# A hybrid diffusion step on one core: the split activations of the dense layers at other SBUF start addresses

## The chip, the cores and the metric

The kernel runs on one core of a Trainium2 chip. The metric is the device time of one execution in microseconds. The program has five instruction streams: PE (matmuls), its weight loads (PEld), DVE, ACT and POOL (elementwise work), and SP, which issues all DMAs. Of the kernel before there are three timed executions, and one more was taken with the hardware profiler.

## The reference

Two layers of a hybrid backbone over 384 tokens (128 of context and 256 latent ones), D_MODEL = 1024, all in float32. Per layer, cut to what matters here:

```
h   = rms_norm(x) * (1 + scale1) + shift1
u   = h @ w_in                          # 1024 -> 11328 columns
y0, y1, y2 = ssd(u), attention(u), mlstm(u)
out = sum_n(sigmoid(g_n) * (y_n @ w_branch[n])) @ w_out
x   = x + gate1 * out
h   = rms_norm(x) * (1 + scale2) + shift2
x   = x + gate2 * ((silu(a) * b) @ w_ffn_out)   # a, b = halves of h @ w_ffn_in
```

At the end there is one more rms_norm. The result must agree with a float32 computation, which decides how the matmuls are done.

## The kernel before, in words

**Dense products.** All activations lie transposed, [128 channels, 8 blocks of channels, 384 tokens]. A dense operand is held as two float32r tiles, an upper part (the value rounded by a copy to float32r) and a lower part (value minus upper part). Weights stream from HBM in pieces of 128x1024 (`raw`) and are split the same way by ACT (`wh`) and by DVE or POOL (`wl`), in `piece` (lines 700 to 729). A product is three matmuls: wh with the upper part, wh with the lower part, wl with the upper part. In the names of the trace the upper and lower parts are HH and HL (inputs of the mixers, of the second of the three branch projections and of the output projection), PH and PL (the first and the third branch projection), A and C (input of the FFN, 386 columns: two more carry the shift). They are all filled by `split_act`, `modulate` and `scaled`.

**Which operand moves.** In `dense_t` (line 736) the weights are stationary, 128 columns each, and the activations stream past, 384 or 386 columns; this is the form of nearly all work. In `dense_n` (line 774; queries, keys, values) the roles are changed: 128 tokens of HH or HL are stationary, and 512 columns of `wh` or `wl` stream. In the second FFN product (line 1553) the moving halves lie in D, E, F, B, HH and HL, by 4, 4, 4, 2, 4 and 4 blocks of the hidden dimension.

**The order.** All calls are recorded first; `Recorder.order` (line 409) then runs a small model of the engines (costs in line 367, priorities set by `urgency`) and writes every engine's instructions in the order that the model finds. Neither the model nor its table of buffers knows an address. `Engines`' instructions are all emitted in line 545, so every row of the trace has that line, and rows are told apart by tiles.

**Addresses.** Each buffer tag is one place in a pool, and pools lie one behind the other in SBUF, per partition in bytes: constants `cp`, pad p1, weights `wp` (raw, wh, wl), pad p2, `bp`, pad p3, `mp`, small buffers `sp`, rings `rp`. `PADS` sets the pads' sizes. `wp` begins at 21760, which is 85 x 256. All tags of `bp` and `mp` have sizes that are multiples of 256 bytes (12288, 6144, 12544, 14336 to 16384 and 15360), and a block of 384 columns is 1536 = 6 x 256 bytes, a row of A or C 448 x 4 = 7 x 256 bytes. So all blocks of one tag begin at one value modulo 256. Before, p2 = 64 puts A to F, PH and PL at 64; p3 = 192 puts HH and HL back to 0.

**Two places used below as measures.** The setup splits some of the first weight pieces not into `wp` but into A and E (`OPEN_HOMES`, line 584), which lie at 64 modulo 256: those matmuls have stationary weights at 64 and HH or HL at 0 as the moving part.

The functions touched and those that call them:

Of the kernel before, what the change touches and what calls it, by code (L numbers as in the profile page):

```python
# [17 lines left out]
D = 1024  # L18
# [47 lines left out]
def stream():  # L66

    s = [(("ada", 0, u), 4) for u in range(4)]
    for l in range(LAYERS):
        early = iter(gates())  # L70
        s += [(("gate", l) + next(early), 1) for _ in range(FIRST_GATES if l else 0)]
        s += [(("dtmg", l), 1)]
        base = [(("in", l, OFF[n] + j * P), 1) for n in ("sx", "sb", "sc") for j in range(2 if n != "sx" else 8)]
        base += [(("inn", l, OFF["aq"] + j * 512), 4) for j in range(3)]
        base += [(("in", l, OFF[n] + j * P), 1) for n in ("mq", "mk") for j in range(8)]
        base += [(("inn", l, OFF["mv"] + j * 512), 4) for j in range(2)]
        base += [(("in", l, OFF[n] + j * P), 1) for n in ("sz", "mo") for j in range(8)]
        main = []
        for i, it in enumerate(base):
            main += [(("gate", l) + next(early), 1) for at in EARLY_GATES[FIRST_GATES if l else 0:] if at == i]  # L80
            main += [it]
        main += [(("br", l, n, j), 1) for n, j in gates()]
        at = len(main) - ADA_OVER

        late = []
        for i in range(KT):
            late += [(("ada", 0, 1, i // 2), 4)] if i % 2 else []
            late += [(("adv", 0, SHIFT2, i), 1), (("adv", 0, GATE2, i), 1)]
        s += main if l else main[:at] + spread(main[at:], late)
        s += [(("out", l, j), 1) for j in range(8)]  # L90
        ff = [((n, l, j), 1) for j in range(FT) for n in ("fa", "fb")]
        fo = [(("fo", l, i), 1) for i in range(FT)]
        if l + 1 < LAYERS:
            blocks = [(("adv", l + 1, place, j), 1) for place in range(6) for j in range(8)]
            n = len(ff) - ADV_FROM
            at = len(blocks) * n // (n + len(fo))
            s += ff[:ADV_FROM] + spread(ff[ADV_FROM:], blocks[:at]) + spread(fo, blocks[at:])
        else:
            s += ff + fo
    return s  # L100
# [33 lines left out]
class Buf:  # L134


    def __init__(self, pool, shape, dtype, tag, bufs, name, ext=None):
        self.pool, self.shape, self.dtype, self.tag, self.bufs, self.name, self.ext = pool, shape, dtype, tag, bufs, name, ext
        self.real = ext
        self.psum = False  # L140
        self.writes, self.reads = [], []
        self.left, self.place, self.ends = 0, 0, {}
# [427 lines left out]
ND, NM, NL = 3, 4, 1  # L570


BIG = ("A", "B", "C", "D", "E", "F", "PH", "PL")
MOVED = ("HH", "HL")
PADS = dict(p1=96, p2=64, p3=192)

ROW = 448
NR = 4
# [17 lines left out]
class Net:  # L596
    def __init__(self, ctx, tc, I, O):
        self.tc = tc
        self.rec = Recorder()
        self.nc = Engines(self.rec)  # L600
        ext = lambda d: {k: View(Buf(None, tuple(v.shape), F32, None, None, k, ext=v)) for k, v in d.items()}
        self.I, self.O = ext(I), ext(O)
        e = ctx.enter_context
        PSUM, DRAM = bass.MemoryType.PSUM, bass.MemoryType.DRAM
        self.pools = {n: e(tc.tile_pool(name=n, bufs=1, **k)) for n, k in (
            ("cp", {}), ("p1", {}), ("wp", {}), ("p2", {}), ("bp", {}), ("p3", {}), ("mp", {}), ("sp", {}), ("rp", {}), ("pd", dict(space=PSUM)), ("pm", dict(space=PSUM)),
            ("pl", dict(space=PSUM)), ("dr", dict(space=DRAM)))}
        self.n = 0
        self.stream = stream()
        self.spos = 0  # L610
        self.ppos = 0
        self.turn = 0
# [7 lines left out]
        return self.buf("cp", name, shape, 1)  # L620

    def slot(self, tag, shape, dt=F32):
        return self.buf("bp" if tag in BIG else "mp" if tag in MOVED else "sp", tag, shape, 1, dt)

    def ring(self, tag, shape, bufs=2, dt=F32):
        return self.buf("rp", tag, shape, bufs, dt)
# [302 lines left out]
    def setup(self):  # L929
# [10 lines left out]
        for k in (0, KT // 2):  # L940
            self.dma(self.x[:, k:k + KT // 2], I["xT"][:, k:k + KT // 2])
        for n, size in PADS.items():
            if size:
# [835 lines left out]
```

## Time and profile before

| | us |
|---|---|
| median of 3 executions | 1867.72 |
| lowest, highest | 1866.60, 1870.51 |
| the profiled execution | 1869.78 |
| its span, first to last instruction | 1868.0 |
| PE busy in it | 1827.6 (98%) |
| weight loads busy | 1716.6 (92%) |
| DVE, ACT, POOL busy | 1411.8, 942.5, 380.6 |

A matmul's duration in the trace is longer than its share of the engine, because the next one starts while it drains. The time that a matmul costs in a run without a pause is the distance between starts: (start of the last minus start of the first) divided by the number of matmuls between. The granted clock was 1.00 in nearly the whole span, which is 2.4 GHz, so 384 columns alone are 160.0 ns.

### The profile page before, as it was taken

The numbers are of one execution on the slowest core, as the hardware profiler recorded it, in microseconds if no ns is written. First come the engines' busy times: TensorE is split into PE (matmuls) and PEld (weight loads), VectorE is DVE, ScalarE is ACT, GpSimd is POOL, SyncE is SP. The second block draws the span as 40 slices with busy tenths as digits, with TensorE's granted clock in tenths as the row PEclk, the third lists the DMA queues.
The fourth block names the chain that finished last, engine by engine and source line by source line (L and its number), as shares of the span: only waits on it lengthen the run. The fifth ranks groups of instructions, "written<-read, shape, count | busy, mean of one in ns | idle before, by whom it ended". The sixth has DMA issues, their size and how long they took to land. (4 is left out here: it accounts for less than half of the span.)

```text
span 1868.0 us, 30198 instructions
## 1 busy us (share of the span) xinstructions
PE 1827.6 (98%) x10888; PEld 1716.6 (92%) x10888; DVE 1411.8 (76%) x2988; ACT 942.5 (50%) x1905; POOL 380.6 (20%) x365
## 2 busy tenths in 40 slices
PE   6999999999999999999999999999999999999997
PEld 5998998788889999999999889977989999999996
DVE  5858866898879889999879788578987567666522
ACT  4555655666533444443356556556665334544431
POOL 0223311232012211214402233112310121000132
PEclk9999999999999999999999999999999999999998
DMA  9466444665398757676764764445644554444441
GB/s 338 143 177 181 134 133 140 149 175 158 123 349 291 238 166 218 219 230 202 232 201 138 177 170 126 139 129 150 190 122 150 172 157 156 129 128 126 124 125 57
DMA packets 118598, 320.42 MB, mean 172 GB/s; under 512 B 13872, under 2 KB 57264, under 8 KB 116528
## 3 DMA queue, kind: packets, MB, share of 16 engines
q1 hardware_dynamic: 118448, 318.49, 55.9%
q8 instruction: 86, 1.41, 0.3%
q14 instruction: 64, 0.52, 0.1%
HBM read 297.64 MB, written 19.75 MB: 170 GB/s over the span
## 5 line engine op out<-in xcount | busy, mean ns | idle before, releaser
L545 ACT ACTIVATE wh<-raw 128x1024 fp32r<-128x1024 f32 x372 | 393.8, 1059 | 524.8 <-PE d L545 454.5
L545 DVE TENSOR_TENSOR wl<-raw,wh 128x1024 fp32r<-128x1024 f32 x350 | 452.8, 1294 | 206.0 <-ACT wh L545 204.9
L545 PE MATMUL d<-HH,wh 128*128 128x384 f32 x1424 | 483.0, 346 | 0.0
L545 PE MATMUL d<-HL,wh 128*128 128x384 f32 x1424 | 466.4, 335 | 0.0
L545 PE MATMUL d<-HH,wl 128*128 128x384 f32 x1360 | 455.9, 335 | 0.0
L545 PEld LDWEIGHTS d<-HH,wh 128*128 128x128 f32 x1424 | 267.1, 188 | 13.8 <-issue 11.3
L545 PEld LDWEIGHTS d<-HL,wh 128*128 128x128 f32 x1424 | 267.0, 188 | 0.7
L545 PEld LDWEIGHTS d<-HH,wl 128*128 128x128 f32 x1360 | 255.3, 188 | 0.0
L545 PE MATMUL d<-A,wh 128*128 128x386 f32 x744 | 252.5, 339 | 0.4 <-DVE sc L545 0.4
L545 PE MATMUL d<-C,wh 128*128 128x386 f32 x744 | 251.2, 338 | 0.0
L545 PE MATMUL d<-A,wl 128*128 128x386 f32 x744 | 251.1, 338 | 0.0
L545 PEld LDWEIGHTS d<-A,wh 128*128 128x128 f32 x744 | 140.6, 189 | 1.1 <-issue 0.7
L545 PEld LDWEIGHTS d<-C,wh 128*128 128x128 f32 x744 | 140.7, 189 | 0.4
L545 PEld LDWEIGHTS d<-A,wl 128*128 128x128 f32 x744 | 140.6, 189 | 0.0
L545 POOL TENSOR_TENSOR sc<-sc,sc 128x126 f32<-128x126 f32 x112 | 61.8, 573 | 314.8 <-DVE sc L545 252.3
L545 POOL TENSOR_TENSOR wl<-raw,wh 128x1024 fp32r<-128x1024 f32 x22 | 55.9, 2543 | 269.5 <-ACT sh L545 190.2
L545 DVE SCALAR_TENSOR_TENSOR PH<-PL,n,cst 128x128 f32<-128x128 f32 x288 | 96.7, 370 | 10.8 <-DMA PL<-rowr 5.0
L545 PE MATMUL d<-wh,HH 128*128 128x512 f32 x240 | 97.8, 407 | 0.0
L545 PE MATMUL d<-wl,HH 128*128 128x512 f32 x240 | 93.9, 391 | 0.0
L545 PE MATMUL d<-wh,HL 128*128 128x512 f32 x240 | 93.7, 391 | 0.0
L545 PE MATMUL d<-PH,wh 128*128 128x384 f32 x256 | 86.7, 339 | 0.0
L545 PE MATMUL d<-PH,wl 128*128 128x384 f32 x256 | 86.2, 337 | 0.0
(283 smaller groups left out, 3200.9 us busy)
## 6 DMA issues: line engine op xcount, KB each, us to landing
raw<-in_ws SPq DMA_DIRECT2D x438, 512.0 KB, 3.8
PL<-rowr SPq DMA_DIRECT2D x48, 384.0 KB, 5.3
gd<-sc SPq DMA_DIRECT2D x48, 192.0 KB, 2.0
pb<-gd SPq DMA_DIRECT2D x48, 192.0 KB, 3.3
A<-in_ws SPq DMA_DIRECT2D x4, 1536.0 KB, 8.1
ex<-rowe SPq DMA_DIRECT2D x32, 128.0 KB, 3.9
ex<-rowe SPq DMA_DIRECT2D x16, 256.0 KB, 5.6
yad<-pb SPq DMA_DIRECT2D x16, 192.0 KB, 3.4
```

Source lines behind the costliest of these rows:

```text
L545: tc.keep_in_program_order(getattr(engines[op.eng], meth)(*[real(a) for a in args], **{k: real(v) for k, v in kw.items()}))
```

## The change

The tags of dense operands get a pool by a table, `HOME`. `bp` keeps B, D, E and F. The upper parts A, HH and PH go to a new pool `hp`, the lower parts C, HL and PL to `lp`. Four pads stand between the pools: p3 grows from 192 to 224 and p4 = 160 is new. By the sizes above, `wp` stays at 0 modulo 256 and `bp` at 64; `hp` begins at 64 + 224 = 288, which is 32 modulo 256, and `lp` at 32 + 160 = 192.

```
-BIG = ("A", "B", "C", "D", "E", "F", "PH", "PL")
-MOVED = ("HH", "HL")
-PADS = dict(p1=96, p2=64, p3=192)
+HOME = dict(B="bp", D="bp", E="bp", F="bp", A="hp", HH="hp", PH="hp", C="lp", HL="lp", PL="lp")
+PADS = dict(p1=96, p2=64, p3=224, p4=160)
...
-("cp", {}), ("p1", {}), ("wp", {}), ("p2", {}), ("bp", {}), ("p3", {}), ("mp", {}), ("sp", {}), ("rp", {}), ...
+("cp", {}), ("p1", {}), ("wp", {}), ("p2", {}), ("bp", {}), ("p3", {}), ("hp", {}), ("p4", {}), ("lp", {}), ("sp", {}), ("rp", {}), ...
...
-        return self.buf("bp" if tag in BIG else "mp" if tag in MOVED else "sp", tag, shape, 1, dt)
+        return self.buf(HOME.get(tag, "sp"), tag, shape, 1, dt)
```

The small buffers and the rings behind move up by 192 bytes in all. On PE, DVE, ACT and SP the two programs have the same instructions in the same order, with the same waits; only buffer numbers and addresses differ. POOL has one instruction more, at its start, where the pads are set to zero. Its list there before (p_6 to p_8 are the pads, `ones` and `silc` are constants):

```order
L545 MEMSET p_6_93 128x24
L545 MEMSET p_7_97 128x16
L545 MEMSET p_8_99 128x48
L545 MEMSET ones_101 128x128
L545 MEMSET silc_103 128x256
```

and with the change:

```order
L545 MEMSET p_6_99 128x24
L545 MEMSET p_7_103 128x16
L545 MEMSET p_8_105 128x56
L545 MEMSET p_9_107 128x40
L545 MEMSET ones_109 128x128
L545 MEMSET silc_113 128x256
```

One pad of 40 columns has come in ahead of `ones`, and the pad before it is 8 columns wider.

## Rows read from the trace of the kernel before

**Rows 1.** The page, part 1: engines' busy time, share of the span, instructions.
```profile
PE 1827.6 (98%) x10888; PEld 1716.6 (92%) x10888; DVE 1411.8 (76%) x2988; ACT 942.5 (50%) x1905; POOL 380.6 (20%) x365
```

**Rows 2.** Busy time by stretches: start:end, length, engines' busy time (instructions), granted clock, DMA.
```profile
540.00:860.00 320.00, 319.58 (x1846) 313.75 (x1846) 292.84 (x461) 136.29 (x249) 68.22 (x44) 1.00 0.72 235
1460.00:1780.00 320.00, 320.00 (x1838) 319.73 (x1837) 201.19 (x292) 141.68 (x252) 33.56 (x25) 1.00 0.46 140
```

**Rows 3.** The page, part 5: matmul groups, count | busy us, mean ns | idle before.
```profile
L545 PE MATMUL d<-HH,wh 128*128 128x384 f32 x1424 | 483.0, 346 | 0.0
L545 PE MATMUL d<-HL,wh 128*128 128x384 f32 x1424 | 466.4, 335 | 0.0
L545 PE MATMUL d<-HH,wl 128*128 128x384 f32 x1360 | 455.9, 335 | 0.0
L545 PE MATMUL d<-A,wh 128*128 128x386 f32 x744 | 252.5, 339 | 0.4 <-DVE sc L545 0.4
L545 PE MATMUL d<-C,wh 128*128 128x386 f32 x744 | 251.2, 338 | 0.0
L545 PE MATMUL d<-A,wl 128*128 128x386 f32 x744 | 251.1, 338 | 0.0
L545 PE MATMUL d<-wh,HH 128*128 128x512 f32 x240 | 97.8, 407 | 0.0
L545 PE MATMUL d<-PH,wh 128*128 128x384 f32 x256 | 86.7, 339 | 0.0
L545 PE MATMUL d<-PL,wh 128*128 128x384 f32 x256 | 86.2, 337 | 0.0
```

**Rows 4.** Timeline of PE, moving HH and HL at 0, weights at 0: start, us.
```profile
247.84 0.33 PE L545 MATMUL d<-HH,wh 128*128 128x384 f32 x1
...
250.96 0.81 PE L545 MATMUL m<-C,D 128*128 128x256 f32 x4
```

**Rows 5.** Timeline of PE, moving PH and PL at 64, weights at 0.
```profile
523.58 0.34 PE L545 MATMUL d<-PH,wh 128*128 128x384 f32 x1
...
525.66 0.34 PE L545 MATMUL d<-PH,wh 128*128 128x384 f32 x1
```

**Rows 6.** Timeline of PE, FFN: moving A and C at 64, 386 columns.
```profile
851.51 0.34 PE L545 MATMUL d<-A,wh 128*128 128x386 f32 x1
...
855.71 0.51 PE L545 MATMUL d<-D,wh 128*128 128x384 f32 x2
```

**Rows 7.** Timeline of PE, `dense_n`: stationary HH and HL at 0, 512 columns.
```profile
153.91 0.39 PE L545 MATMUL d<-wh,HH 128*128 128x512 f32 x1
...
157.31 0.39 PE L545 MATMUL d<-wh,HH 128*128 128x512 f32 x1
```

**Rows 8.** Timeline of PE, stationary weights in E at 64, moving HH, HL at 0.
```profile
48.26 0.34 PE L545 MATMUL m<-HH,E 128*128 128x384 f32 x1
...
52.50 0.33 PE L545 MATMUL d<-HH,wh 128*128 128x384 f32 x1
```

**Rows 9.** Timeline of PE, HH and HL resuming behind three transposes.
```profile
241.11 0.49 PE L545 MATMUL m<-cst,pb 128*128 128x128 f32 x3
241.35 0.42 PE L545 MATMUL d<-HH,wh 128*128 128x384 f32 x1
241.61 0.33 PE L545 MATMUL d<-HL,wh 128*128 128x384 f32 x1
...
242.50 0.33 PE L545 MATMUL d<-HH,wh 128*128 128x384 f32 x1
```

**Rows 10.** Timeline of PE, second FFN product: B (64), then HH (0), then HL (0).
```profile
872.89 0.51 PE L545 MATMUL d<-B,wh 128*128 128x384 f32 x2
...
873.93 0.51 PE L545 MATMUL d<-HH,wh 128*128 128x384 f32 x2
...
875.51 0.51 PE L545 MATMUL d<-HL,wh 128*128 128x384 f32 x2
```

**Rows 11.** Groups of ACT: two squares of one shape, written to `sc` (128) and `nacc` (96).
```profile
L545 ACT ACTIVATE sc<-PH 128x384 f32<-128x384 f32 x35 | 17.6, 516 | 22.0 <-DVE PH L545 21.9
L545 ACT ACTIVATE nacc<-PH 128x384 f32<-128x384 f32 x5 | 2.6, 516 | 6.0 <-DMA PH<-in_xT 3.0 <-DVE PH L545 3.0
```

**Rows 12.** Groups of POOL: the memset of `ones`.
```profile
L545 POOL MEMSET ones<- 128x128 f32 x1 | 0.2, 204 | 0.0
```

More of the change, by code (lines that the diff above doesn't have):

```diff
@@ L605, in __init__ @@
         self.pools = {n: e(tc.tile_pool(name=n, bufs=1, **k)) for n, k in (
-            ("cp", {}), ("p1", {}), ("wp", {}), ("p2", {}), ("bp", {}), ("p3", {}), ("mp", {}), ("sp", {}), ("rp", {}), ("pd", dict(space=PSUM)), ("pm", dict(space=PSUM)),
+            ("cp", {}), ("p1", {}), ("wp", {}), ("p2", {}), ("bp", {}), ("p3", {}), ("hp", {}), ("p4", {}), ("lp", {}), ("sp", {}), ("rp", {}), ("pd", dict(space=PSUM)), ("pm", dict(space=PSUM)),
             ("pl", dict(space=PSUM)), ("dr", dict(space=DRAM)))}
```

## The prediction

> **What bounds the kernel now.** I read the page's busy shares first: PE is busy 1827.6 of 1868.0 us, DVE 76% [rows 1]. Then the busy time by stretches: in the two long stretches of FFN and branch work PE has no idle time worth naming, at a granted clock of 1.00, while DVE has 91% in one and 63% in the other [rows 2]. So only what a matmul costs PE counts, and since the change moves no instruction on PE, ACT, DVE or SP, only an address can change that cost. The third view is the list of matmul groups, for their counts [rows 3]; the fourth the timeline of PE, where the distance between starts shows what one really costs.
>
> **What one dense matmul costs, by the addresses of its operands.** Steady stretches, no pause in them:
> - moving at 0, weights at 0: 18 matmuls from 247.84 to 250.96 us, 173.3 ns each [rows 4];
> - moving at 64, weights at 0: 12 in 2.08 us, 173.3 ns [rows 5];
> - moving at 64, 386 columns: 24 in 4.20 us, 175.0 ns [rows 6];
> - 512 columns of weights moving, HH and HL stationary, both at 0: 15 in 3.40 us, 226.7 ns [rows 7];
> - moving at 0, weights at 64: 24 in 4.24 us, 176.7 ns [rows 8].
>
> At 2.4 GHz the columns alone take 160.0, 160.8 and 213.3 ns. The rest is 13.3 ns at 384 and at 512 columns, so it belongs to the change of weights and not to the columns. [...] The start of the moving part, 0 or 64, makes no difference; the start of the stationary part, 64 in place of 0, costs 3.4 ns.
>
> [...]
>
> **The change part by part.**
> - *Upper parts moving, at 32.* HH, A and PH from 0 or 64: 1424 + 1360 + 744 + 744 + 256 + 256 = 4784 matmuls (A with wl and PH with wl are as many as with wh) [rows 3]. No row has a moving operand at 32. The nearest, 0 and 64, lie on both sides and are equal, so I take 0. Bounds: one step of 3.4 ns up or down each, 16.3 us.
> - *Lower parts moving, at 192.* HL, C and PL: 1424 + 744 + 256 = 2424 [rows 3], and 64 of HL with wl in the second FFN product, 2488. Taken as 0, by the same rows. Bounds: 3.4 ns each, 8.5 us either way.
> - *HH and HL stationary in `dense_n`, at 32 and 192.* 3 x 240 matmuls [rows 3]. The one row with a stationary part off 0 is that of E [rows 8], and I take its price: 720 x 3.4 = +2.4 us. Bounds: nothing, if it is the distance of the two operands that decides, and twice as much, 4.9 us.
> - *Resuming behind other work.* Where HH and HL resume behind transposes, the first matmul takes 0.26 us to the next start, and the five that follow take 0.89 us in place of 0.867, so 23 ns more [rows 9]. In the second FFN product the step from B (64) to HH (0) shows the same without any pause: six matmuls of B take 1.04 us, as they should, the nine from HH on 1.58 in place of 1.56, and then the rhythm is back [rows 10]. So a moving part at 0 needs some 20 ns to fall into step. How often: the mean of the first matmul in each block of three is 346 ns against 335 [rows 3], and one that resumes has 420 [rows 9], so (346 - 335) x 1424 / (420 - 335) = about 184 times; with 23 ns each 4.2 us at stake. Whether 32 behaves as 0 does (nothing gained) or as 64 (all of it), no row tells; I take half, -2.1 us. Bounds: -4.2 and, if two different starts in turn make it twice as long, +4.2.
> - *The opening's matmuls on A and E.* A moves from 64 to 32 and E stays: 48 matmuls, at most 0.2 us. Nothing.
> - *Small buffers and rings, 192 bytes on.* The same square on ACT takes 516 ns into a buffer at 128 and into one at 96 [rows 11], so a start off a multiple of 64 costs ACT nothing; ACT, DVE and POOL lie beside PE anyway. If that cover were gone, DVE's 91% [rows 2] would be the first to show it. 0.
> - *One memset more on POOL.* 40 columns against 128 in 204 ns [rows 12]; POOL is busy 20% of the span and starts with nothing else to do. 0, at most 0.2 us.
>
> Sum against the profiled execution: 1869.78 + 2.4 - 2.1 = 1870.1. That execution lies 2.06 us above the median of the timed ones, so the forecast for the median is 1868.1 us: no change that can be told. What a measurement of this kernel tells from no change is about 0.2%, 3.7 us; the three executions span 3.9 us. With the bounds of the two small terms alone (-4.2 to +9.1) the likeliest case reaches from 1863.5 to 1876.8.
>
> **The rivals.**
> 1. *The distance of the two operands decides, not where the weights begin: slower.* In the row of E the moving part lies 64 below the weights, which is 192 above, modulo 256; and that is just where the lower parts now lie over the weights. Then every one of 2488 lower matmuls pays 3.4 ns: +8.5 us, with `dense_n` +2.4 and half of the term of resuming gone as above, 1876.5 us; with the upper parts paying as well, 1892.8. It decides from 1.5 ns per lower matmul on. For it: the only slow row is also the only one with that distance, and the step in [rows 10] shows that the relation of streams matters at least for a moment. Against: 0 and +64 are exactly alike, which a conflict that depends on distance would not lead one to expect. A stronger form, that each step between two starts costs its 20 ns, would give some 2488 x 20 ns = 50 us; but there the rhythm settles within six matmuls, and with a step at each matmul it would be a new steady rhythm, which no row prices.
> 2. *The 13.3 ns are no constant, and the new starts cut them: faster.* The row of E shows that they change with addresses, by 3.4 ns. If starts that differ between upper part, lower part and weights keep the reads out of each other's way, the lower matmuls alone would give 2488 x 3.4 = 8.5 us, 1859.6; all 7272 would give 24.7 us, 1843.4. For it: the rest is the same at any number of columns, as it would be if loading 128 weights held up the stream, and before, upper and lower part never began at different values. Against: two starts were seen, with exactly the same rest.
> 3. *The addresses do nothing at all, not even in `dense_n`*: 1867.7, inside the forecast's range.
>
> **How the numbers follow.** Forecast and rival 3 together 0.46, rival 1 0.25, rival 2 0.29. Of the first, some 0.04 fall below 1864 by the term of resuming and 0.03 above 1871.5 by that of `dense_n`, and a part of 0.01 of rival 2 is too small to be told. So faster by over 0.2%: 0.32; within 0.2%: 0.40; slower: 0.28. The range has to hold rival 2 but for its far end, and rival 1 with lower parts and part of the upper ones: 1847 to 1885. The likeliest case's own range stands above.
>
> **What would show it.** In the timeline after, a steady stretch of HH and HL and one of A and C: 173.3 and 175.0 ns per matmul say that the moving part's start is free; 176 to 177 in every third say rival 1, anything below 172 rival 2. `dense_n` shows 230 ns if the stationary part's start counts, 226.7 if not. Behind transposes, five matmuls in 0.87 us say that a start at 32 falls into step as one at 64 does. The forecast is wrong if steady distances differ from these by more than a nanosecond, since 7272 of them make 7 us.

## The result and the profile after

The changed kernel takes 1881.16 us (median of 6 executions, 1878.51 to 1883.62), the kernel before 1869.57 us (6 executions, 1866.60 to 1871.54): a ratio of 1.0059, with a 95% interval of 1.0048 to 1.0070. So it is slower by 11.6 us. The forecast was 1868.1 us, no change. The time lies within the stated range of 1847 to 1885, in the case that had a chance of 0.28, but outside the likeliest case's own range of 1863.5 to 1876.8.

The page of the changed kernel, part 1, answers to [rows 1]:
```profile
PE 1837.5 (98%) x10888; PEld 1724.8 (92%) x10888; DVE 1411.5 (75%) x2988; ACT 943.8 (50%) x1905; POOL 382.3 (20%) x366
```
PE is busy for 9.9 us more with the same 10888 matmuls; the other engines stand still. PE's idle time, span less busy time, is 40.4 us before and 40.1 after. So the time is not in a new wait: the matmuls themselves cost more.

The two stretches of [rows 2], now:
```profile
540.00:860.00 320.00, 319.30 (x1829) 313.27 (x1828) 290.90 (x461) 135.15 (x245) 65.79 (x43) 1.00 0.72 235
1460.00:1780.00 320.00, 320.00 (x1821) 319.73 (x1820) 202.21 (x293) 141.00 (x250) 31.11 (x24) 1.00 0.47 140
```
The granted clock is 1.00 in both, as before, and PE is as full as before, but 17 matmuls fewer fit into each 320 us (1829 against 1846, 1821 against 1838). That is 0.9% in stretches where PE does almost nothing but dense products.

The matmul groups (name, count | busy us, mean ns), which answer to [rows 3]:
```profile
L545 PE MATMUL d<-HH,wh 128*128 128x384 f32 x1424 | 485.9, 348 | 0.0
L545 PE MATMUL d<-HL,wh 128*128 128x384 f32 x1424 | 470.8, 338 | 0.0
L545 PE MATMUL d<-HH,wl 128*128 128x384 f32 x1360 | 457.1, 336 | 0.0
L545 PE MATMUL d<-A,wh 128*128 128x386 f32 x744 | 254.7, 342 | 0.7 <-DVE sc L545 0.7
L545 PE MATMUL d<-A,wl 128*128 128x386 f32 x744 | 250.2, 336 | 0.0
L545 PE MATMUL d<-wh,HH 128*128 128x512 f32 x240 | 98.5, 411 | 0.0
```
No group stands out: most rise by 1 to 4 ns, and one falls. What one matmul costs is read from the distance between starts. In the timeline of PE, the same four kinds of stretch as in [rows 4], [rows 6], [rows 7] and [rows 8]: HH and HL; A and C; `dense_n`; the opening's product on the weights in E.
```profile
247.61 0.33 PE L545 MATMUL d<-HH,wh 128*128 128x384 f32 x1
...
250.77 0.38 PE L545 MATMUL m<-C,D 128*128 128x256 f32 x1
...
855.06 0.34 PE L545 MATMUL d<-A,wh 128*128 128x386 f32 x1
...
858.23 0.34 PE L545 MATMUL d<-D,wh 128*128 128x384 f32 x1
...
153.96 0.39 PE L545 MATMUL d<-wh,HH 128*128 128x512 f32 x1
...
157.45 0.40 PE L545 MATMUL d<-wh,HH 128*128 128x512 f32 x1
...
48.07 0.51 PE L545 MATMUL m<-HH,E 128*128 128x384 f32 x2
...
51.19 0.34 PE L545 MATMUL m<-HH,E 128*128 128x384 f32 x1
```
18 matmuls of HH and HL take 3.16 us, 175.6 ns each (before 173.3); 18 of A and C 3.17 us, 176.1 (175.0); 15 of `dense_n` 3.49 us, 232.7 (226.7); and 18 on E, where neither the weights nor their start has changed, 3.12 us, 173.3 (176.7). So three became dearer and one cheaper.

Starts are recorded to the nanosecond, so the rhythm within such a stretch can be shown. Distances between successive starts, in ns, in the stretches of [rows 4] (before) and at 247.61 us (after):
```
before  HH,wh HL,wh HH,wl ...   173 174 173 173 174 173 173 174 173 173 174 173
after   HH,wh HL,wh HH,wl ...   172 178 173 180 177 174 171 178 173 180 178 173
```
The twelve take 2080 ns before and 2107 after: twice 13.3 ns more, so 13.3 ns in every six. They are spread over several distances and don't come in one piece.

To compare kernels I add up such losses over all dense matmuls: the distance to the next start, less the steady distance of before at the same number of columns, which is 173.3 ns at 384 [rows 4], 175.0 at 386 [rows 6] and 226.7 at 512 [rows 7]. What is over 25 ns is a wait for other work or the first matmul behind one, and is left out (23.1 us before, 22.9 after). The sum is 3.7 us before and 17.6 us after, 13.9 us more; the medians differ by 11.6, with an interval of 9.0 to 13.1, and the spans of the two profiled executions by 9.6. The two profiled executions differ in one thing more, the granted clock. Besides the end of both, it is 0.50 in two stretches before and in one after (busy time by stretches, as in [rows 2]; the third line is after):
```profile
24.60:31.40 6.80, 5.90 (x45) 4.96 (x35) 4.68 (x13) 5.04 (x8) 0.00 (x0) 0.50 1.03 432
536.60:540.00 3.40, 3.40 (x16) 1.69 (x9) 3.27 (x7) 0.00 (x0) 0.00 (x0) 0.50 0.90 321
24.10:27.50 3.40, 2.97 (x57) 2.51 (x46) 0.58 (x2) 1.53 (x3) 0.00 (x0) 0.50 1.09 455
```
The matmuls outside the sum spend 7.8 us in these stretches before and 3.1 after, and in all take 3.5 us less after than before. So the two spans understate what the starts cost; the losses leave such matmuls out.

The first of these stretches also gives an estimate of what the columns alone cost. Timeline of PE before, at the clock of 0.50:
```profile
28.81 0.53 PE L545 MATMUL d<-HL,A 128*128 128x384 f32 x1
...
30.73 0.53 PE L545 MATMUL d<-HL,A 128*128 128x384 f32 x1
```
Six matmuls of 384 columns take 1.92 us, 320.0 ns each. Half of that is an estimate of the columns alone at 1.00: 160.0 ns, 2.4 columns a ns. From 384 to 512 columns the distance at 1.00 grows by 53.4 ns for 128 columns [rows 4, 7], the same rate. The views give the clock as a share only; what the forecast calls 2.4 GHz is this rate.

### The profile page after: what moved, and what is told of

It is laid out like the page before. It is cut to its first block, busy times and chain, and to the rows that moved or that the text cites. A ratio compares the mean times of both kernels' runs of the same rounds, so it can differ in the third digit from the quotient of the medians.

```text
span 1877.6 us, 30199 instructions
## 1 busy us (share of the span) xinstructions
PE 1837.5 (98%) x10888; PEld 1724.8 (92%) x10888; DVE 1411.5 (75%) x2988; ACT 943.8 (50%) x1905; POOL 382.3 (20%) x366
## 5 line engine op out<-in xcount | busy, mean ns | idle before, releaser
L545 PEld LDWEIGHTS d<-HH,wh 128*128 128x128 f32 x1424 | 266.7, 188 | 13.9 <-issue 11.3
L545 DVE SCALAR_TENSOR_TENSOR PH<-PL,n,cst 128x128 f32<-128x128 f32 x288 | 97.9, 374 | 10.8 <-DMA PL<-rowr 5.1
L545 PE MATMUL d<-PL,wh 128*128 128x384 f32 x256 | 86.5, 338 | 0.0
```

What stands on the lines that cost most here:

```text
L545: tc.keep_in_program_order(getattr(engines[op.eng], meth)(*[real(a) for a in args], **{k: real(v) for k, v in kw.items()}))
```

## The experiments

Four theories were set against each other. **D**: each distance of the moving part's start from the weights' start, modulo 256 bytes, has its price (the prediction's first rival). **S**: it is the alternation between two different starts that costs (its "stronger form"). **A**: the start itself is dear, wherever the weights lie. **R**, formed after the first four runs: the starts decide which steady rhythms there are, and the way into a stretch picks one of them. Starts are given modulo 256 bytes, as upper/lower part relative to the weights; the edits are of `PADS` unless another is shown.

The measured times stand in one table, with the losses by operand from each kernel's own trace:

| kernel | starts | us | against before | HH HL PH PL | A C | `dense_n` | losses, us |
|---|---|---|---|---|---|---|---|
| before | 0/0, 64/64 | 1869.6 to 1869.8 | | 2.4 | 0.2 | 1.1 | 3.7 |
| changed | 32/192 | 1881.16 | 1.0048 to 1.0070 | 10.8 | 2.9 | 3.9 | 17.6 |
| e1_all_64_on | 32/192 | 1881.91 | 1.0053 to 1.0079 | 10.7 | 2.9 | 3.9 | 17.5 |
| e2_both_192 | 192/192 | 1876.38 | 1.0022 to 1.0048 | 6.7 | 1.4 | 1.8 | 10.0 |
| e3_both_32 | 32/32 | 1875.57 | 1.0016 to 1.0042 | 3.4 | 3.7 | 4.1 | 11.2 |
| e4_both_128 | 128/128 | 1882.22 | 1.0054 to 1.0082 | 11.9 | 3.7 | 3.7 | 19.5 |
| f1_upper64_lower0 | 64/0 | 1878.05 | 1.0031 to 1.0059 | 3.5 | 6.2 | 4.0 | 13.6 |
| f2_all_64 | 64/64 | 1869.09 | 0.9987 to 1.0008 | 0.2 | 0.3 | 4.2 | 4.8 |
| g1_before_grouped | 0/0, 64/64 | 1877.52 | 1.0039 to 1.0078 | 2.4 | 2.9 | 1.2 | 6.4 |
| g2_64_0_grouped | 64/0 | 1878.45 | 1.0052 to 1.0095 | 3.8 | 1.0 | 3.4 | 8.2 |
| g3_after_grouped | 32/192 | 1882.40 | 1.0075 to 1.0120 | 5.3 | 3.5 | 3.9 | 12.8 |

The first column of times is on one chip for e1 to e4 and on another for f1 and f2 (before there 1869.8 both times); the g kernels ran on a third, where before took 1865.16.

**All operands 64 bytes further on.**
```
-PADS = dict(p1=96, p2=64, p3=224, p4=160)
+PADS = dict(p1=160, p2=64, p3=224, p4=160)
```


> The changed kernel with all its dense operands 64 bytes further on: weights at 64 modulo 256, branch blocks at 128, upper parts at 96, lower parts at 0. Every distance between two operands is as in the changed kernel. Theory D (the distance between the moving part and the weights decides) and theory S (a step of the stream between two different starts costs): as changed, steady HH/HL 175.6 ns, dense_n 231 ns, about 1881 us. Theory A (the start itself decides, as weights at 64 alone): every dense matmul at 176.7 ns or more, 7272 x 1.1 to 3.4 ns on top, 1889 us or more, or, if only moving parts at 32 and 192 were dear, back at 1870.

Measured 1881.91 us with the losses of the changed kernel in every column. A shift of all operands by the same 64 bytes changes nothing (17.5 us of losses for 17.6); A falls.

**One start for upper and lower part: 192, 32, 128.**
```
+PADS = dict(p1=96, p2=64, p3=128, p4=0)     # both at 192
+PADS = dict(p1=96, p2=64, p3=224, p4=0)     # both at 32
+PADS = dict(p1=96, p2=64, p3=64, p4=0)      # both at 128
```


> Weights at 0, upper and lower parts both at 192 modulo 256: no step between different starts inside a stretch, but every moving part 64 below the weights. Theory D: every dense matmul as E's in the opening of the kernel before, 176.7 ns, 7272 x 3.4 = +24 us over before, 1894 us. Theory S: 173.3 ns and about 1870 us. Theory A: the price of a start at 192 on all: also above the changed kernel, so it is told from D only by the first run.

> Weights at 0, upper and lower parts both at 32 modulo 256. Theory D: the distance 32 has its own price, and in the changed kernel the upper matmuls took 1.4 ns over 173.3 on the mean, so 174.5 to 175 ns on all here, 7272 x 1.4 = +10 us, about 1880 us. Theory S: one start only, 173.3 ns, 1870 us (1872 if dense_n keeps its 230 ns).

> Weights at 0, upper and lower parts both at 128 modulo 256. Theory D: in the changed kernel's opening the lower part lies 128 above its weights (192 over 64) and takes 173.3 ns, so 128 is free: 173.3 ns, 1867 to 1870 us, less by up to 4 us if no time is lost on resuming. Theory S: one start, 1870 us. Theory A: 128 has no row; with the price of 192, 1894 us.

Measured: +6.6, +5.8 and +12.4 us. D expected +24, +10 and nothing, S nothing in all three: neither has them. The trace of the kernel with both at 192 shows why no price per distance can be found. Timeline of PE, two stretches of HH and HL one behind the other, with equal starts:
```profile
247.19 0.34 PE L545 MATMUL d<-HH,wh 128*128 128x384 f32 x1
...
249.79 0.34 PE L545 MATMUL d<-HH,wh 128*128 128x384 f32 x1
...
250.31 0.81 PE L545 MATMUL m<-C,D 128*128 128x256 f32 x4
...
251.50 0.34 PE L545 MATMUL d<-HH,wh 128*128 128x384 f32 x1
...
254.15 0.34 PE L545 MATMUL d<-HH,wh 128*128 128x384 f32 x1
```
The first 15 matmuls take 2.60 us, 173.3 ns each; four small matmuls come between; and the next 15 take 2.65 us, 176.7 ns each. The same kind of instructions with the same starts modulo 256 has two rhythms. At 32/32 there are two as well (173.3 and 176.7; one stretch of 194 matmuls stays in the slow one to its end), at 128/128 one of 176.0: its distances are 174 174 175 182 175, in all 13.3 ns more in five. So 128/128 is as dear as the changed kernel, with equal starts.

**All pairs of starts, alone.** A kernel with dense products only; its core:
```
+for lead in (0, 128, 264):               # columns of one matmul ahead of the stretch
+    for u, l in PAIRS:                   # 64 pairs of starts
+        stretch(product(u, l), 384, lead)   # 24 matmuls (wh,u) (wh,l) (wl,u) ..., then a wait for ACT
```


> Only dense products, none of the rest of the kernel (its outputs are zeros): weights at 0, 24 matmuls of 384 columns in the order upper, lower, upper, for all 64 pairs of starts (0 to 224 in steps of 32, modulo 256), each pair three times, entered behind a wait, behind one matmul of 128 columns and behind one of 264; then stretches of 18 with 512 columns of weights moving. Theory R (starts decide which steady rhythms there are, each with one extra slip of 13.3 ns in a whole number of matmuls, and the way in picks one): pairs 0/0 and 64/64 173.3 ns, 32/32 173.3 or 176.7, 128/128 176.0, 192/192 two or three of 173.3, 174.7, 176.7, 32/192 175.6, and one pair may differ with its entry. Theory D (each distance has a price): a pair costs (2 x price of upper + price of lower) / 3, whatever the entry. Theory S (steps cost): all pairs with equal starts are cheaper than all with different ones.

Measured, ns per matmul over the last 18 distances of each stretch entered behind a wait (rows: start of the upper part, columns: of the lower):
```
        0     32     64     96    128    160    192    224
  0 173.3  173.3  174.1  176.7  175.6  175.6  175.2  175.6
 32 174.1  173.3  174.4  175.4  175.6  173.3  175.6  175.6
 64 174.1  175.1  173.5  175.6  173.4  175.6  174.8  173.5
 96 176.7  175.9  173.3  176.7  176.3  175.7  176.7  175.6
128 175.4  175.6  175.4  175.3  175.5  174.4  175.6  175.3
160 174.8  175.6  175.1  175.6  175.6  176.7  175.6  175.6
192 173.3  175.5  173.3  177.8  177.8  175.6  174.8  175.6
224 174.4  174.8  175.7  173.9  173.3  176.7  175.4  173.9
```
The floor is 173.3 ns (nothing is below 173.1 with any way in); 32/192 has the 175.6 of the changed kernel. Equal starts are not always cheap (96/96, 128/128), and some different ones are at the floor (192/0, 32/160). With the other two ways in, 160/160 falls from 176.7 to 173.3 and 192/192 rises from 174.8 to 176.7. `dense_n`'s order, with 512 columns of weights moving, is at 226.7 only where both stationary parts are at 0; with both at 192 it has 228.8, and the nine other pairs tried 231.1 to 234.6. That fits R, and neither D nor S in a pure form.

**Two starts that are each free, alternating; and both at the better one.**
```
+PADS = dict(p1=96, p2=64, p3=0, p4=192)     # 64/0
+PADS = dict(p1=96, p2=64, p3=0, p4=0)       # 64/64
```


> Weights at 0, upper parts at 64, lower parts at 0: both starts that were free in the kernel before, but different from each other. Theory D: 173.3 ns, about 1868 to 1871 us. Theory S: every matmul is a step of the stream, as in the changed kernel: 175 ns or more, about 1880 us. Theory R leaves it open: a mixed pair is a rhythm of its own.

> Weights at 0, upper and lower parts all at 64, as PH, PL, A and C in the kernel before. All theories: 173.3 ns in every stretch of HH and HL; the 1.1 us that these lose before in stretches of 174 to 175 ns are gone. dense_n has its stationary part at 64 over moving weights at 0: 230 ns by D, +2.4 us. Sum 1868 to 1871 us, not told from before.

64/0 costs 8.3 us, though 64 and 0 are both free in the kernel before [rows 4, 5]: as S has it, and D falls. 64/64 is not told from before. It has the pools of the changed kernel, so the new layout by itself is not what costs. Its products are at the floor everywhere (losses 0.2 and 0.3 us), but what HH and HL gain, 2.2 us, `dense_n` loses, 3.1 us; its timeline there has 15 in 3.50 us, 233.3 ns:
```profile
153.43 0.39 PE L545 MATMUL d<-wh,HH 128*128 128x512 f32 x1
...
156.93 0.40 PE L545 MATMUL d<-wh,HH 128*128 128x512 f32 x1
```

**The same pairs with 2 steps in 24 matmuls in place of 16.** Alone:
```
+m = product(u, l)
+stretch(m[0::3] + m[2::3] + m[1::3], 384, lead)   # 16 matmuls on the upper part, then 8 on the lower
```


> As the map of pairs, dense products alone (outputs are zeros), but each stretch of 24 takes its 16 matmuls with the upper part first and then its 8 with the lower part: one step between starts in place of 16. Then 32/32 and 192/192 entered behind single matmuls of 64 to 352 columns, and seven pairs in stretches of 72 in the old order. Theory S (alternating between two starts is what costs, beside what each start costs alone): pair 64/0 falls from 174.1 to 173.3 ns, 32/192 from 175.6 to the 173.3 of 32 in its 16 and 173.3 to 176.7 in its 8. Theory R without S (a pair has its rhythm whatever the order): 64/0 and 32/192 as in the map. Ways in: 32/32 at 173.3 in most and 176.7 in some, 192/192 at 174.7 or 176.7. Stretches of 72 keep one period from the tenth matmul to the last.

In the 64/0 pair the 16 now take 173.3 ns each; the 8 at 0 need their six matmuls to settle (distances 170 175 178 185 176 181, 25 ns over), as [rows 10] had it. In 32/192 the 16 are at 173.4, and the 8 at 192 take 176.7, as 192/192 can alone. So the steps cost in both pairs, as S has it: with 16 steps in 24 matmuls 32/192 has 175.6 on the mean, with two about 174.5, and at the floor it would have 173.3. The ways in, with 192/192: timeline of PE behind one matmul of 128, of 256 and of 352 columns:
```profile
672.75 0.33 PE L767 MATMUL d<-HH,wh 128*128 128x128 f32 x1 [0.33 <-ACT ev L770]
...
673.84 0.34 PE L769 MATMUL d<-HH,wl 128*128 128x384 f32 x1
...
676.96 0.34 PE L769 MATMUL d<-HH,wl 128*128 128x384 f32 x1
...
711.72 0.39 PE L767 MATMUL d<-HH,wh 128*128 128x256 f32 x1 [0.33 <-ACT ev L770]
...
712.82 0.34 PE L769 MATMUL d<-HH,wl 128*128 128x384 f32 x1
...
715.96 0.34 PE L769 MATMUL d<-HH,wl 128*128 128x384 f32 x1
...
741.34 0.42 PE L767 MATMUL d<-HH,wh 128*128 128x352 f32 x1 [0.33 <-ACT ev L770]
...
742.49 0.34 PE L769 MATMUL d<-HH,wl 128*128 128x384 f32 x1
...
745.67 0.34 PE L769 MATMUL d<-HH,wl 128*128 128x384 f32 x1
```
18 matmuls take 3.12, 3.14 and 3.18 us: 173.3, 174.7 (from unrounded starts) and 176.7 ns. Only the matmul ahead differs, so the way in picks the rhythm. 32/32 does the same (173.3 behind 96 to 256 and 320 columns, 176.6 to 176.8 behind 64, 288 and 352). In stretches of 72 the period stays to the end: 173.3 for 0/0, 64/64 and 32/32, 175.6 for 32/192, 174.1 for 64/0.

In the whole kernel:
```
-            for k in range(KT):
-                self.mms(..., [(hi[:, k], hh[:, k]), (hi[:, k], hl[:, k]), (lo[:, k], hh[:, k])], ...)
+            todo = [(hi[:, k], hh[:, k]) for k in range(KT)] + [(lo[:, k], hh[:, k]) for k in range(KT)]
+            todo += [(hi[:, k], hl[:, k]) for k in range(KT)]
+            for k in range(KT):
+                self.mms(..., todo[3 * k:3 * k + 3], ...)
```


> The kernel before with the order inside each dense product changed: 16 matmuls on the upper part, then 8 on the lower part, in place of upper, lower, upper. Starts as before (0 and 64, upper and lower alike), so no theory expects a difference in steady stretches: 173.3 ns, 1867 to 1873 us. It is the measure for the two that follow.

> Uppers at 64, lowers at 0, with the grouped order. Theory S: the sum over 173.3 and 175.0 ns of the products in the alternating order, 9.4 us, falls below 2 us; the 720 of dense_n, which still alternate, keep their 4 us: 1870 to 1872 us. Theory R without S: as with the alternating order, 1878 us.

> The changed kernel (uppers at 32, lowers at 192) with the grouped order. Theory S: uppers as where both are at 32 (0.7 ns over the floor for HH, 1.7 for A), lowers as where both are at 192 (1.3 and 0.6): together 1 ns on 7272 matmuls in place of 2, 1874 to 1877 us. Theory R without S: as changed, 1881 us.

The order itself costs 12.4 us with the starts of before, against the expectation. The losses explain 2.7 of it and longer waits between dense matmuls 2.3 (25.4 us for 23.1). Part of it is new: a product now needs all eight blocks of the upper part in its first eight matmuls, and PE, which in this trace is idle for 46.9 us in place of 40.4, waits for ACT to write them, for 4.3 us in all (us, times, longest). No dense product does so before.
```profile
PE d L545 <- ACT HH L545: 2.6, 4, 1.1
PE d L545 <- ACT A L545: 1.7, 1, 1.7
```
The rest was not followed up. Against this measure, 64/0 now costs 0.9 us in place of 8.3, and 32/192 costs 4.9 in place of 11.6. But each grouped kernel has four executions that spread over 6 to 8 us, so for 32/192 the times alone hardly tell what the order saved; the losses from the traces have to. Without `dense_n`, which still alternates, the losses of 64/0 over the measure are -0.4 us (in the old order +7.1), those of 32/192 +3.6 (+11.2). The measure flatters them: its own A and C, at 64/64, fell into a slow rhythm in half of their matmuls, 2.9 us in place of 0.2. With 0.2 there the figures are +2.3 and +6.3. So the steps carry most of the cost of 64/0, though its products still lose 4.8 us where S expected under 2, and about half (4.9 to 7.6 of 11.2 us) of that of 32/192. The rest is near what the single starts lose where both parts share one: the upper parts 4.7 us here and 4.0 at 32/32, the lower parts 4.1 and 2.5 at 192/192.

**What the 13.3 ns are.** 64 and 32 stationary columns in place of 128, and 256 and 512 moving:
```
+nc.tensor.matmul(ps[0:c, 0:n], (wl if x == 2 else wh)[:, k * P:k * P + c], m[:, o:o + n], ...)
```


> Dense products alone once more (outputs are zeros), 24 matmuls to a stretch in the order upper, lower, upper, with 128, 64 and 32 stationary columns in place of 128 alone, moving 384, 256 and 512 columns, for the pairs 0/0, 64/64, 128/128, 96/96, 192/192, 32/192 and 64/0. Theory W (the 13.3 ns over the columns, and each slip of 13.3 ns, are the fetch of 128 weights): 64 weights make them 6.7 ns, so 64/64 takes 166.7 ns and the slow pairs slip by 6.7; 32 weights 163.3 ns. Theory F (a fixed turnaround of 32 cycles): 173.3 ns and slips of 13.3 whatever the weights. With 256 moving columns 64/64 takes 120.0, with 512 it takes 226.7 ns at 128 weights by both.

Timeline of PE: 32 weights under 384 columns (0/0), then 128 weights under 256 columns (192/192):
```profile
99.35 0.34 PE L794 MATMUL d<-HH,wh 128*32 128x384 f32 x1
...
102.47 0.34 PE L794 MATMUL d<-HH,wh 128*32 128x384 f32 x1
...
146.23 0.28 PE L794 MATMUL d<-HH,wh 128*128 128x256 f32 x1
...
148.27 0.28 PE L794 MATMUL d<-HH,wh 128*128 128x256 f32 x1
```
At 0/0, 32 weights leave 173.3 ns as they are (3.12 us for 18): at 384 columns W falls. They do change which rhythm another pair has (64/64 takes 173.3 ns with 128 weights and 175.6 with 32). But 256 columns take 113.3 ns at 192/192 (2.04 us for 18), 6.7 over the columns at the 2.4 a ns found above (106.7): F, a fixed 13.3, falls as well. The other six pairs with 128 weights take 117.8 to 120.0 there; 0/0 takes 119.7, and 113.3 with 64 and with 32 weights, so at 256 columns the number of weights does count. What the constant is stays open.

## Why the forecast missed inside its range, step by step

The range held because it was 38 us wide and was drawn to hold rival 1 with part of the upper parts. The likeliest case, that the new starts are free for moving operands, is not what happened.

- **Moving parts at 32 and at 192, both taken as 0: this step failed.** By operand the losses rose by 4.2 us for the uppers (HH 1.6, A 1.9, PH 0.7) and by 7.0 for the lowers (HL 5.2, C 0.8, PL 1.0). The prediction read a price per start from stretches in which every matmul had one and the same start [rows 4, 5], and concluded from two equal prices that a third start is free. It is not, even without alternation: the losses of the products rise by 4.5 us where both parts are at 32 and by 5.5 where both are at 192. And about half of the cost of 32/192 comes from two starts in turn, which stood in no row. The prediction said so ("a new steady rhythm, which no row prices") and still gave that form no bounds of its own. The stretches after answer its own test: 175.6 and 176.1 where 173.3 and 175.0 were to say that a start is free.
- **`dense_n`, +2.4 us:** right in sign, and in size by luck: the losses rose by 2.8 us. The steady rhythm rose by 6.0 ns (232.7 for 226.7) and not by 3.4, but before had lost 1.1 us already. Nor was it for the reason taken. Its 3.4 ns came from E's product [rows 8] as the price of weights at 64, and that product runs at 173.3 after, with the weights where they were.
- **Resuming, -2.1 us:** the sign can't be told from the rest. Behind the transposes five matmuls take 0.87 us, as was forecast for a start that falls into step:
```profile
240.88 0.49 PE L545 MATMUL m<-cst,pb 128*128 128x128 f32 x3
241.13 0.42 PE L545 MATMUL d<-HH,wh 128*128 128x384 f32 x1
241.39 0.34 PE L545 MATMUL d<-HL,wh 128*128 128x384 f32 x1
...
242.26 0.34 PE L545 MATMUL d<-HH,wh 128*128 128x384 f32 x1
```
  (0.89 in [rows 9]); but the steady rhythm behind is slower. At 64/64, where nothing else costs, the term shows: HH, HL, PH and PL lose 0.2 us in place of 2.4.
- **Small buffers, the memset, the opening: 0.** Right: ACT 943.8 for 942.5 us, POOL 382.3 for 380.6, both beside PE.
- **Rival 1** was nearest, with 1876.5 to 1892.8 around the time, but only half its mechanism holds: a distance has no price, as both parts at 192 show (+6.6 us where it says 24). Its stronger form had the right kind of cause at the wrong size: if all of a pair's cost is put on its steps, 1.2 ns per step at 64/0 (0.8 x 3 / 2) and 3.4 ns at 32/192, not 20.
- **Rival 2** had 0.29, and nothing stood for it but two equal rows. With 384 columns and 128 weights the floor is 173.3 ns in the map and in every kernel; the kernel before stands 3.7 us above its floor, so a placement of starts that keeps to this floor could give no more than 0.2%. Nor is the rest the same at any number of columns, as was read from two sizes: at 256 columns it is 6.7 ns at 192/192 and up to 13.3 with the other pairs. That it belongs to the change of weights, no run shows: with 384 columns at 0/0 it is 13.3 ns for 128, 64 and 32 weights.
- **Rival 3**, that the addresses do nothing, falls with the map, whose 64 pairs take from 173.3 to 177.8 ns.

Of the 13.9 us of losses 11.6 appear between the medians. They did not go into waits that PE has anyway, since its idle time hardly changed (40.4 and 40.1 us); in the two profiles the clock hides some of them (the matmuls outside the sum spend 7.8 us at 0.50 before and 3.1 after), and the rest of the difference stays open.

## What to carry to other kernels

In this kernel, with PE busy for 98% of the span, other starts of the operands cost 0.6% (11.6 us): measure each start in the place where it is used. A start that was free alone (64, 173.3 ns [rows 5]) was dear in alternation (64/0, +8.3 us) and as the stationary part (64 in `dense_n`, 233.3 ns for 226.7), and one start for both parts was no guarantee: 64/64 was as good as before, 128/128 as dear as the changed kernel (+12.4 us). Read such prices as distances between starts over ten or more matmuls, to the nanosecond: here the mean durations rose by 1 to 4 ns in most groups and fell in one, and PE's idle time moved by 0.3 us. And a row for one configuration is no bound for another that alternates between two.

## What the runs showed of the hardware

- The means of many steady rhythms are the floor plus 13.3 ns in a whole number of matmuls: 4 (176.7, 192/192 in the whole kernel), 5 (176.0, 128/128), 6 (175.6, the changed kernel), 18 (174.1, 64/0 alone), and with 512 columns 2 (233.3, 64/64) or 3 (231.1, in the map). Not all fit (234.6 at 512 columns, in the map), and single distances need not show a slip: in the 176.7 of 192/192 each is 176 to 178.
- Two or three rhythms held at one set of addresses (192/192: 173.3, 174.7, 176.7), and a stretch kept the one it had entered: for 72 matmuls alone, and for 194 with both parts at 32 in the whole kernel.
- As far as tried, only differences of starts counted: 64 bytes more on all operands changed nothing (17.5 us of losses for 17.6). That 256 bytes is the period was taken and not tested by itself; A and C, whose blocks lie 7 x 256 bytes apart, keep 175.0 ns before [rows 6], which fits it.
- What stands over the columns at 2.4 a ns was 13.3 ns at 384 columns for 32, 64 and 128 weights (0/0). At 256 columns it was 13.0 ns with 128 weights and 6.7 with 64 or 32 (0/0), and 6.7 with 128 at 192/192.
